# Full-height score and broadcast matmuls, and a last gated merge whose gate products run two tiles ahead

## The chip, the cores and the metric

The kernel runs on one core of a Trainium2 chip. The metric is the device time of one execution in microseconds (us), the median of several runs. The engines are TensorE (PE in the profile; its weight loads are listed apart as PEld), VectorE (DVE), ScalarE (ACT), GpSimd (POOL) and SyncE (SP), which issues the transfers.

## What is computed

A trunk of two layers over 256 latent tokens and 256 context tokens of width 1024, all in fp32. Each layer normalises and modulates its input, runs four branches of width 256 (a bidirectional mLSTM, differential attention, a Fourier mix and a spatial-gating MLP), projects each branch back to 1024, weighs it with a sigmoid gate, sums the four and projects the sum; then comes a gated feed-forward block. The parts that the change touches:

```python
def step(carry, inp):                      # mLSTM, one chunk of 128 tokens
    C, n, m = carry
    qc, kc, vc, ic, fc = inp
    b = jnp.cumsum(fc, axis=-1)
    dmat = jnp.where(tril, b[..., :, None] - b[..., None, :] + ic[..., None, :], -jnp.inf)
    inter = b + m[..., None]
    m_t = jnp.maximum(inter, jnp.max(dmat, axis=-1))
    wt = jnp.exp(dmat - m_t[..., None])
    ...
    s = jnp.einsum('bhtd,bhsd->bhts', qc, kc) * wt
    num = a[..., None] * jnp.einsum('bhvk,bhtk->bhtv', C, qc) + jnp.einsum('bhts,bhsv->bhtv', s, vc)

def merge(branches, gate_pre, w_branch, w_out):
    br = jnp.stack(branches, axis=2)
    y = jnp.einsum('bsgc,gcd->bsgd', br, w_branch)
    gt = jax.nn.sigmoid(gate_pre.reshape(gate_pre.shape[:2] + (N_BRANCH, D_MODEL)))
    return jnp.einsum('bsgd,bsgd->bsd', gt, y) @ w_out
```

The last layer computes its query side for the latent tokens alone.

## The kernel before

**Number form.** TensorE has no full-speed fp32 product here. A value is split into a high part (cast to the type fp32r) and a low part (what the cast dropped), and a product is three matmuls: high x high (line 135), high x low (136), low x high (137). `wload` (line 111) brings a weight tile of 128x1024 in over SyncE (`raw`), casts it on ScalarE (`hi`, line 122) and subtracts on VectorE or GpSimd (`lo`, line 131). There are four such buffers, and two more in layer 1.

**Tokens.** Activations lie with channels on the partitions and tokens along the columns. Layer 0 works on `TQ` = 512 columns (latent and context tokens), layer 1 on 256.

**mLSTM scores.** For each of the four heads of a layer the program builds weights `W` on VectorE and ScalarE from a broadcast tile `nb`, computes scores of queries and keys on TensorE, multiplies both on VectorE (`mulw`, line 1052), and sums over tokens with the values (`nu`, line 1092, plain fp32). A head is 64 channels, half the partitions. `split_pair` (lines 923 to 937) therefore packs the two parts of the key into one tile `k2`: the high part in the head's 64 partitions, the low part in the other 64. `q2` holds the query's high part twice. One 128-row matmul `k2` x `q2` then gives two of the three products (line 942), and a second one of 64 rows, `k2`'s high part x `ql`, the third (line 943). `ql`, the query's low part, is one tile for a pair of heads, each in its own 64 partitions. A head has four pairs of such matmuls: in layer 0 two with 256 columns and two with 512, in layer 1 four with 256.

**Broadcast.** `NM` holds a running minimum per head and direction, in rows 0 to 3 and 32 to 35. `NMr` (lines 998 to 1000) is its high and low part on 36 partitions. Line 1029 spreads one row over all 128 partitions: the left operand is a column of an identity matrix (`idr`) repeated 128 times. There are four such matmuls for a head, with `TQ` columns.

**Merge.** `merge(g)` goes over eight output tiles `m` of 128 channels: gate product `gt` (24 matmuls on `w_gate`), tanh on ScalarE into `sig`, branch product `yb` (6 matmuls on `w_branch`), `sig` times `yb`, sum into `za`. Three merges are done as a generator that `fill(n)` advances by `n` half tiles between the steps of the branches: branches 2, 3 and 0; the last, branch 1 (the attention), runs at the end of the mixer and also writes `z`, the operand pair of the output projection (`split_out`: high part on ScalarE, low part on VectorE). `finish_heads` (line 710 on) normalises a branch's heads and queues `turn_heads`, which transposes the result on TensorE (`pt`, line 725, plain fp32) and splits it into the operands `bh` (line 680, ScalarE) and `bl` (line 681, VectorE) of the branch product. `finish_now` runs what is queued. In the layer's end (lines 1341 to 1349) the program does two steps of merge 0, then `finish_now`, then the rest of merge 0, then the last merge.

**Order and buffers.** A scheduler sets the order of the instructions of each engine by the priority in which the program wrote them, and moves what is ready. Of PSUM's eight banks three are for `gt`, `yb` and the projections, five for the rest (`nb`, scores, `nu`, `pt`). In layer 0 VectorE also works off a list of adaLN rows (`junk`, line 232) for the feed-forward block, one with each merge tile.

Of the kernel before, what the change touches and what calls it, by code (L numbers as in the profile page):

```python
# [10 lines left out]
F32 = mybir.dt.float32  # L11
F32R = mybir.dt.float32r
I32 = mybir.dt.int32
AF = mybir.ActivationFunctionType
# [5 lines left out]
KD = 8  # L20
# [15 lines left out]
def trunk_kernel(ctx: ExitStack, tc: tile.TileContext, I, out):  # L36
# [25 lines left out]
    def mmb(name="mm"):  # L62
        return mmp.tile([128, 512], F32, tag="mm", name=name)
# [584 lines left out]
    def layer(l):  # L648
# [15 lines left out]
        with ExitStack() as es:  # L664
# [41 lines left out]
            def finish_heads(g, hs, t2, wmul, wbc, post):  # L706
# [22 lines left out]

                fins.append(turn_heads)  # L730

            def merge(g, first=False, final=False):
                wb = None
                for m in range(KD):

                    wt = wload(I["w_gate"][l, m, g])
                    if m % 4 == 0:
                        wb = wload(I["w_branch"][l, g, m // 4])
                    ps = mmb("gt")
                    gemm(ps[:, :TQ], wt, h, 0, TQ, ks=range(4), last=False)  # L740
                    if not final:
                        yield

                    gemm(ps[:, :TQ], wt, h, 0, TQ, ks=range(4, KD), w0=4, first=False)
                    sig = wk.tile([128, 512], F32, tag="sig", name="sig")[:, :TQ]
                    last_sig[0] = ins_of(nc.scalar.activation(out=sig, in_=ps[:, :TQ], func=AF.Tanh, scale=0.5))
                    ps = mmb("yb")
                    gemm(ps[:, :TQ], wb, br[g], 0, TQ, ks=range(2), w0=2 * (m % 4))
                    o = za[m] if first else sig
                    at = nc.vector.scalar_tensor_tensor(out=o, in0=sig, scalar=1.0, in1=ps[:, :TQ], op0=ALU.add,  # L750
                                                        op1=ALU.mult)
                    if not first:
                        (nc.vector if final else nc.gpsimd).tensor_tensor(out=za[m], in0=za[m], in1=sig, op=ALU.add)
                    if final:
                        split_out(z[m], za[m], 0.5)
                    tick(1, ins_of(at))
                    yield
# [10 lines left out]
            def fill(n):  # L768
                for _ in range(n):
                    while units:  # L770
                        if next(units[0], 0) is None:
                            break
                        units.pop(0)
# [110 lines left out]
            def mlstm():  # L884
# [4 lines left out]
                Bt = w2.tile([128, T], F32, name="mlB", tag="mlB")  # L889
                NM = w2.tile([128, T], F32, name="mlNM")  # L890
                sp = []
                uem = w2.tile([128, 2, 4, 64], F32, name="uem")
                nc.gpsimd.memset(Bt, 0.0)
                nc.gpsimd.memset(NM, 0.0)
                qk = []
# [27 lines left out]
                def split_pair(p):  # L923

                    aq, ak = qk[2 * p:2 * p + 2]
                    for hh in range(2):
                        o, x_ = slice(64 * hh, 64 * hh + 64), slice(64 - 64 * hh, 128 - 64 * hh)
                        if hh == 0:
                            ql = w2.tile([128, TQ], F32R, name="ql", tag="ql")
                        q2 = w2.tile([128, TQ], F32R, name="q2", tag=f"q2{hh}")  # L930
                        k2 = w2.tile([128, T], F32R, name="k2", tag=f"k2{hh}")
                        nc.scalar.copy(q2[o], aq[o])
                        nc.scalar.copy(k2[o], ak[o])
                        nc.scalar.copy(q2[x_], aq[o])
                        nc.vector.tensor_tensor(out=k2[x_], in0=ak[o], in1=k2[o].bitcast(F32), op=ALU.subtract)
                        nc.vector.tensor_tensor(out=ql[o], in0=aq[o], in1=q2[o].bitcast(F32), op=ALU.subtract)
                        sp.append((q2, k2, ql))

                def score(ps, j, n):
                    q2, k2, ql = sp[hd]  # L940
                    s = slice(j * 128, (j + 1) * 128)
                    nc.tensor.matmul(ps, k2[:, s], q2[:, 0:n], start=True, stop=False)
                    nc.tensor.matmul(ps, k2[pr, s], ql[pr, 0:n], start=False, stop=True)

                qk_tiles(0, CFG["qa"][l])

# [48 lines left out]
                                        op0=ALU.mult)  # L995
                nc.vector.tensor_copy(uem[:, 1, :, 0:36], pv_[:, 1, :, 0:36])

                NMr = [w.tile([128, T], F32R, name=f"NMr{i}", tag=tg)[0:36] for i, w, tg in ((0, w2, "mlB"), (1, w3, "mlU"))]
                nc.vector.tensor_copy(NMr[0][:, :TQ], NM[q, :TQ])
                nc.vector.tensor_tensor(out=NMr[1][:, :TQ], in0=NM[q, :TQ], in1=NMr[0][:, :TQ].bitcast(F32), op=ALU.subtract)  # L1000


                wo = w2.tile([128, NTQ, 256], F32, name="wo")
# [17 lines left out]
                for hd in range(4):  # L1021
# [3 lines left out]
                    for d in range(2):  # L1025
                        row = hd + 32 * d
                        nb = aux("nb")
                        for i in range(2):
                            nc.tensor.matmul(nb[:, :TQ], idr[0:36, row:row + 1].to_broadcast([36, 128]), NMr[i][:, :TQ],
                                             start=(i == 0), stop=(i == 1))  # L1030
                        W = w2.tile([128, 9 if last else 10, 128], F32, name="W", tag="W", bufs=CFG["W"])
                        mask = cst[:, C_MF:C_MF + 128] if d == 0 else cst[:, C_MB:C_MB + 128]
                        u = lambda j: uem[:, 0, j, row:row + 1]
                        for j in range(NTQ):
                            nc.vector.scalar_tensor_tensor(out=W[:, j, :], in0=nb[:, j * 128:(j + 1) * 128], scalar=u(j),
                                                           in1=mask, op0=ALU.add, op1=ALU.add)
                        nc.scalar.activation(out=W[:, 0:NTQ, :], in_=W[:, 0:NTQ, :], func=AF.Exp)
                        for j in (2, 3):
                            nc.scalar.activation(out=W[:, 2 * j:2 * j + 2, :].rearrange("p a b -> p (a b)"), in_=nb[:, 0:256],
                                                 func=AF.Exp, bias=u(j), scale=1.0)  # L1040
                        sj, tj = (0, 1) if d == 0 else (1, 0)
                        nc.scalar.activation(out=W[:, 8, :], in_=nb[:, tj * 128:(tj + 1) * 128], func=AF.Exp, bias=u(sj), scale=1.0)
                        if not last:
                            nc.scalar.activation(out=W[:, 9, :], in_=nb[:, (2 + tj) * 128:(3 + tj) * 128], func=AF.Exp,
                                                 bias=u(2 + sj), scale=1.0)
                        Ws.append(W)
# [292 lines left out]
                            for m in range(CFG["na"] if last else 16, 40))  # L1339
            diff(*(diff_tiles() if last else dqk))  # L1340
            es3.close()
            fill(CFG["f3"][l])
            finish_now()
            fill(64)
            G1 = mod_scale(vec, mod, 2, 1, False, ns)
            g1 = row_of(G1, "t1", RS) if last else None
            open_z()
            units.append(merge(1, final=True))
            fill(64)
            turn[1] = CFG["tw1"] if last else CFG["tw"]  # L1350
            es1.close()
# [237 lines left out]
def ins_of(i):  # L1589
    return i.ins if hasattr(i, "ins") else i  # L1590
# [79 lines left out]
```

## Time and profile before

| | us |
|---|---|
| median of three runs | 1425.84 |
| lowest and highest run | 1424.82, 1427.07 |
| the profiled execution, its own time | 1426.35 |
| its span in the trace | 1424.2 |
| TensorE busy in the span | 1356.0 (95%) |
| VectorE, ScalarE, GpSimd busy | 858.6, 621.5, 848.1 |

The span is what the hardware profiler saw from the first instruction to the last; some 2.2 us of the execution's time lie around it. Busy time of TensorE includes the overlap of a matmul with the next: a row's length is longer than the distance to the next row's start. Two stretches of mLSTM heads lie at 137 to 196 us (layer 0) and 990 to 1042 us (layer 1). The last merges run around 392 to 460 us and 1153 to 1190 us.

### The profile page before, as it was taken

How to read it: one execution, taken by the hardware profiler on the slowest of the kernel's cores; microseconds unless marked ns; L12 is line 12 of the kernel's file. 1: busy time of each engine (PE TensorE's matmuls, PEld its weight loads, DVE VectorE, ACT ScalarE, POOL GpSimd, SP SyncE). 2: the span in 40 equal slices, each digit the busy share in tenths (PEclk: the TensorE clock that was granted, in tenths of full speed). 3: DMA queues.
4: the chain of work that ended last, by engine and by line, in shares of the span. 5: the costliest groups of instructions: out<-in, count | busy, mean ns of one | idle time of the engine just before them, and what ended most of it. 6: DMA issues, size and time to landing. Idle time of an engine off the chain costs nothing.

```text
span 1424.2 us, 22769 instructions
## 1 busy us (share of the span) xinstructions
PE 1356.0 (95%) x8514; PEld 1201.4 (84%) x8514; DVE 858.6 (60%) x1554; ACT 621.5 (44%) x1098; POOL 848.1 (60%) x974
## 2 busy tenths in 40 slices
PE   8899999999999979999799999798999989899998
PEld 6597789888878969888588889797899988899997
DVE  4738655888785475599876643767637632533323
ACT  4445425443423555423231333466536544555543
POOL 1534133456764676567465545775356889678895
PEclk9999999999999999999899999998999999999999
DMA  9322123333443443465577533433224445355552
GB/s 345 133 103 76 45 69 124 133 134 134 162 149 113 149 158 110 143 227 192 206 248 256 186 123 104 132 122 113 90 75 134 136 161 180 118 192 193 182 188 74
DMA packets 61934, 210.55 MB, mean 148 GB/s; under 512 B 7144, under 2 KB 9728, under 8 KB 61568
## 3 DMA queue, kind: packets, MB, share of 16 engines
q1 hardware_dynamic: 61824, 209.10, 43.2%
q8 instruction: 67, 1.10, 0.3%
q14 instruction: 43, 0.35, 0.1%
HBM read 208.01 MB, written 1.06 MB: 147 GB/s over the span
## 4 chain that ended last, share of the span: by engine, by line
PE 53%; DVE 4%; POOL 3%; issue 2%; ACT 1%; DMA 1%; DVEq 0%; ACTq 0%; SPq 0%; POOLq 0%
PE ug L135 4%; PE ug L136 4%; PE ug L137 4%; PE ua L135 4%; PE ua L136 4%; PE ua L137 4%; PE o L135 3%; PE o L136 3%; PE o L137 3%; PE gt L135 2%; PE gt L137 2%; PE gt L136 2%; POOL lo L131 2%; PE ty L135 2%; PE ty L136 2%
## 5 line engine op out<-in xcount | busy, mean ns | idle before, releaser
L131 POOL TENSOR_TENSOR lo<-raw,hi 128x256 fp32r<-128x256 f32 x814 | 697.6, 889 | 409.9 <-ACT hi L122 383.9
L122 ACT CAST hi<-raw 128x1024 fp32r<-128x1024 f32 (+2 forms) x284 | 293.6, 1036 | 332.8 <-PE ua L136 76.9
L135 PE MATMUL gt<-hh,hi 128*128 128x512 f32 (+1 forms) x512 | 177.5, 347 | 0.0
L131 DVE TENSOR_TENSOR lo<-raw,hi 128x1024 fp32r<-128x1024 f32 (+2 forms) x79 | 120.7, 1527 | 90.2 <-ACT hi L122 90.2
L137 PE MATMUL gt<-hh,lo 128*128 128x512 f32 (+1 forms) x512 | 173.1, 338 | 0.0
L136 PE MATMUL gt<-hl,hi 128*128 128x512 f32 (+1 forms) x512 | 172.6, 337 | 0.0
L135 PE MATMUL ug<-hh,hi 128*128 128x256 f32 (+1 forms) x384 | 126.2, 329 | 11.7 <-DVE ca L1454 11.7
L232 DVE SCALAR_TENSOR_TENSOR ar<-ar,scb 128x1024 f32<-128x1024 f32 x80 | 123.0, 1542 | 18.4 <-DMA ar<-w_adaT 17.6
L136 PE MATMUL ug<-hl,hi 128*128 128x256 f32 (+1 forms) x384 | 125.5, 327 | 0.0
L135 PE MATMUL ua<-hh,hi 128*128 128x256 f32 (+1 forms) x384 | 124.5, 324 | 0.9 <-ACT hh L301 0.9
L137 PE MATMUL ug<-hh,lo 128*128 128x256 f32 (+1 forms) x384 | 125.2, 326 | 0.0
L136 PE MATMUL ua<-hl,hi 128*128 128x256 f32 (+1 forms) x384 | 124.1, 323 | 0.1
L137 PE MATMUL ua<-hh,lo 128*128 128x256 f32 (+1 forms) x384 | 124.0, 323 | 0.0
L135 PEld LDWEIGHTS gt<-hh,hi 128*128 128x128 f32 x512 | 96.9, 189 | 13.4 <-issue 2.5
L137 PEld LDWEIGHTS gt<-hh,lo 128*128 128x128 f32 x512 | 96.9, 189 | 10.7
L136 PEld LDWEIGHTS gt<-hl,hi 128*128 128x128 f32 x512 | 97.2, 190 | 9.7
L135 PEld LDWEIGHTS ug<-hh,hi 128*128 128x128 f32 x384 | 74.3, 193 | 18.5 <-issue 10.2
L135 PE MATMUL o<-fh,hi 128*128 128x256 f32 (+1 forms) x240 | 81.0, 338 | 0.0
L136 PE MATMUL mm<-lo,hh 128*128 128x256 f32 x272 | 78.8, 290 | 1.9 <-DVE lo L131 1.9
L136 PE MATMUL o<-fl,hi 128*128 128x256 f32 (+1 forms) x240 | 80.5, 336 | 0.0
L137 PE MATMUL o<-fh,lo 128*128 128x256 f32 (+1 forms) x240 | 80.5, 335 | 0.0
L135 PE MATMUL mm<-hi,hh 128*128 128x256 f32 x272 | 79.3, 292 | 0.0
(309 smaller groups left out, 3252.2 us busy)
## 6 DMA issues: line engine op xcount, KB each, us to landing
raw<-w_up SPq DMA_DIRECT2D x92, 512.0 KB, 3.6
ar<-w_adaT SPq DMA_DIRECT2D x80, 512.0 KB, 4.2
raw<-w_gate SPq DMA_DIRECT2D x64, 512.0 KB, 3.5
raw<-w_tm SPq DMA_DIRECT2D x24, 512.0 KB, 3.5
raw<-w_dr SPq DMA_DIRECT2D x22, 512.0 KB, 3.5
raw<-w_dn SPq DMA_DIRECT2D x20, 512.0 KB, 3.7
ada_w<-w_ada SPq DMA_DIRECT2D x16, 512.0 KB, 8.4
raw<-w_branch SPq DMA_DIRECT2D x16, 512.0 KB, 3.7
```

Source lines behind the costliest of these rows:

```text
L122: nc.scalar.copy(hi[:, :n], raw[:, :n])
L131: e.tensor_tensor(out=lo[:, s], in0=raw[:, s], in1=hi[:, s].bitcast(F32), op=ALU.subtract)
L135: nc.tensor.matmul(ps, a[0], b[0], start=start, stop=False)
L136: nc.tensor.matmul(ps, a[0], b[1], start=False, stop=False)
L137: return nc.tensor.matmul(ps, a[1], b[0], start=False, stop=stop)
L232: nc.vector.scalar_tensor_tensor(out=raw if st == ns - 1 else junk, in0=raw, scalar=0.5, in1=scb[:, st, :], op0=ALU.mult, op1=ALU.mult, ac ...
```

## The change

Three things are done together.

1. The second score matmul takes all 128 rows of `k2`, and `ql` is 128 rows high with zeros in the half that isn't the head's. For that there are two `ql` tiles per layer, one for each head of a pair, both made once; GpSimd writes the zeros ahead of the heads. The second pair no longer waits to overwrite a shared `ql`.
2. `NMr` has all 128 partitions and the broadcast takes all 128 rows of `idr`'s column. `uem` shrinks from 64 to 36 columns.
3. Merge 0 is finished first. The last merge becomes `merge_last`: the gate product and tanh of tile `m` are issued two tiles ahead of its branch product, and the first two gates stand ahead of the head transposes.

```diff
+            def merge_last(g):
+                sigs, wbs = {}, {}
+
+                def gate(m):
+
+                    wt = wload(I["w_gate"][l, m, g])
+                    ps = mmb("gt")
+                    gemm(ps[:, :TQ], wt, h, 0, TQ)
+                    sigs[m] = wk.tile([128, 512], F32, tag="sig", name="sig")[:, :TQ]
+                    last_sig[0] = ins_of(nc.scalar.activation(out=sigs[m], in_=ps[:, :TQ], func=AF.Tanh, scale=0.5))
+
+                def out(m):
+
+                    if m % 4 == 0:
+                        wbs[0] = wload(I["w_branch"][l, g, m // 4])
+                    ps = mmb("yb")
+                    gemm(ps[:, :TQ], wbs[0], br[g], 0, TQ, ks=range(2), w0=2 * (m % 4))
+                    sig = sigs.pop(m)
+                    at = nc.vector.scalar_tensor_tensor(out=sig, in0=sig, scalar=1.0, in1=ps[:, :TQ], op0=ALU.add,
+                                                        op1=ALU.mult)
+                    nc.vector.tensor_tensor(out=za[m], in0=za[m], in1=sig, op=ALU.add)
+                    split_out(z[m], za[m], 0.5)
+                    tick(1, ins_of(at))
+
+                ahead = 2
+                for m in range(KD + ahead):
+                    if m >= ahead:
+                        out(m - ahead)
+                    if m < KD:
+                        gate(m)
+                    yield
...
-                uem = w2.tile([128, 2, 4, 64], F32, name="uem")
+                qls = [w2.tile([128, TQ], F32R, name=f"ql{hh}", tag=f"ql{hh}") for hh in range(2)]
+                for hh in range(2):
+                    nc.gpsimd.memset(qls[hh][64 - 64 * hh:128 - 64 * hh].bitcast(F32), 0.0)
+                uem = w2.tile([128, 2, 4, 36], F32, name="uem")
...
-                        if hh == 0:
-                            ql = w2.tile([128, TQ], F32R, name="ql", tag="ql")
+                        ql = qls[hh]
...
-                    nc.tensor.matmul(ps, k2[pr, s], ql[pr, 0:n], start=False, stop=True)
+                    nc.tensor.matmul(ps, k2[:, s], ql[:, 0:n], start=False, stop=True)
...
-                NMr = [w.tile([128, T], F32R, name=f"NMr{i}", tag=tg)[0:36] for i, w, tg in ((0, w2, "mlB"), (1, w3, "mlU"))]
-                nc.vector.tensor_copy(NMr[0][:, :TQ], NM[q, :TQ])
-                nc.vector.tensor_tensor(out=NMr[1][:, :TQ], in0=NM[q, :TQ], in1=NMr[0][:, :TQ].bitcast(F32), op=ALU.subtract)
+                NMr = [w.tile([128, T], F32R, name=f"NMr{i}", tag=tg) for i, w, tg in ((0, w2, "mlB"), (1, w3, "mlU"))]
+                nc.vector.tensor_copy(NMr[0][:, :TQ], NM[:, :TQ])
+                nc.vector.tensor_tensor(out=NMr[1][:, :TQ], in0=NM[:, :TQ], in1=NMr[0][:, :TQ].bitcast(F32), op=ALU.subtract)
...
-                            nc.tensor.matmul(nb[:, :TQ], idr[0:36, row:row + 1].to_broadcast([36, 128]), NMr[i][:, :TQ],
+                            nc.tensor.matmul(nb[:, :TQ], idr[:, row:row + 1].to_broadcast([128, 128]), NMr[i][:, :TQ],
...
-            fill(CFG["f3"][l])
+            fill(64)
+            units.append(merge_last(1))
+            fill(2)
             finish_now()
-            fill(64)
             G1 = mod_scale(vec, mod, 2, 1, False, ns)
             g1 = row_of(G1, "t1", RS) if last else None
             open_z()
-            units.append(merge(1, final=True))
             fill(64)
```

In layer 0 the transposes `pt` move on TensorE. Before, they stand in the middle of a gate of merge 0 (`gt_3955`):

```order
L135 MATMUL gt_3955<-hh3_130,hi_3951 128x512
L136 MATMUL gt_3955<-hl3_131,hi_3951 128x512
L137 MATMUL gt_3955<-hh3_130,lo_3952 128x512
L725 MATMUL pt_3968<-cst_93,fsq_3902 128x128 x2
L725 MATMUL pt_3973<-cst_93,fsq_3902 128x128 x2
L725 MATMUL pt_3978<-cst_93,fsq_3911 128x128 x2
L725 MATMUL pt_3983<-cst_93,fsq_3911 128x128 x2
L135 MATMUL gt_3955<-hh4_132,hi_3951 128x512
```

After, on TensorE at the same step, they stand behind the second gate of the last merge (`gt_4088`), and the first branch product of the last merge (`yb_4165`) begins right behind them:

```order
L135 MATMUL gt_4088<-hh7_138,hi_4084 128x512
L136 MATMUL gt_4088<-hl7_139,hi_4084 128x512
L137 MATMUL gt_4088<-hh7_138,lo_4085 128x512
L725 MATMUL pt_4115<-cst_93,fsq_3904 128x128 x2
L725 MATMUL pt_4120<-cst_93,fsq_3904 128x128 x2
L725 MATMUL pt_4125<-cst_93,fsq_3913 128x128 x2
L725 MATMUL pt_4130<-cst_93,fsq_3913 128x128 x2
L135 MATMUL yb_4165<-bh0_2050,hi_4158 128x512
L135 MATMUL gt_4186<-hh0_124,hi_4182 128x512
L136 MATMUL gt_4186<-hl0_125,hi_4182 128x512
L137 MATMUL gt_4186<-hh0_124,lo_4183 128x512
L136 MATMUL yb_4165<-bl0_2051,hi_4158 128x512
```

The transposes have moved 96 matmuls back. `bh0` is written by the first and the third of the four casts, 256 columns each.

On ScalarE of layer 0 those casts stand, before, behind the tanh of an earlier gate (`gt_3886`):

```order
L122 CAST hi_4087<-raw_4085 128x1024
L746 ACTIVATE sig_3934<-gt_3886 128x512
L680 CAST bh0_2048<-pt_3968 128x256
L680 CAST bh1_2050<-pt_3973 128x256
L680 CAST bh0_2048<-pt_3978 128x256
L680 CAST bh1_2050<-pt_3983 128x256
```

After, on ScalarE, they stand behind the tanh of the gate just ahead of the transposes, and behind the cast of a weight tile (`hi_4281`) whose buffer is `gt_4088`'s:

```order
L122 CAST hi_4230<-raw_4228 128x1024
L741 ACTIVATE sig_4080<-gt_4055 128x512
L122 CAST hi_4281<-raw_4279 128x1024
L741 ACTIVATE sig_4113<-gt_4088 128x512
L680 CAST bh0_2050<-pt_4115 128x256
L680 CAST bh1_2052<-pt_4120 128x256
L680 CAST bh0_2050<-pt_4125 128x256
L680 CAST bh1_2052<-pt_4130 128x256
```

What moved: a weight cast and a tanh that both need `gt_4088` now stand between the transposes and their casts. In layer 1 the order is the same, with one cast for each of `bh0` and `bh1`, and two matmuls of a row sum (line 407) between the transposes and the first branch product.

## Rows read from the trace of the kernel before

**Rows 1.** The page, part 1: busy us (share of the span) and instructions.
```profile
PE 1356.0 (95%) x8514; PEld 1201.4 (84%) x8514; DVE 858.6 (60%) x1554; ACT 621.5 (44%) x1098; POOL 848.1 (60%) x974
```

**Rows 2.** The list of waits: us in total, times, longest us.
```profile
PE pt L725 <- DVE fsq L718: 6.5, 3, 3.8
...
DVE junk L232 <- DMA ar<-w_adaT: 9.8, 8, 3.9
```

**Rows 3.** TensorE's timeline, layer 0, head 0: start us, us, engine, line, operation.
```profile
137.64 0.28 PE L137 MATMUL mm<-hi,hl 128*128 128x256 f32 x1
...
139.31 0.40 PE L136 MATMUL gt<-hl,hi 128*128 128x512 f32 x1
...
141.83 0.28 PE L942 MATMUL SL<-q,k 128*128 128x256 f32 x1
142.04 0.38 PE L943 MATMUL SL<-ql,k 64*128 64x256 f32 x1
142.35 0.38 PE L942 MATMUL SL<-q,k 128*128 128x256 f32 x1
...
145.02 0.40 PE L136 MATMUL gt<-hl,hi 128*128 128x512 f32 x1
```

**Rows 4.** The weight loads' timeline of the same head.
```profile
141.60 0.19 PEld L942 LDWEIGHTS SL<-q,k 128*128 128x128 f32 x1
142.04 0.18 PEld L943 LDWEIGHTS SL<-ql,k 64*128 64x128 f32 x1 [0.25 <-issue]
```

**Rows 5.** TensorE's timeline, layer 1, head 0, around its scores.
```profile
996.80 0.28 PE L942 MATMUL SL<-q,k 128*128 128x256 f32 x1
...
999.42 0.28 PE L136 MATMUL gt<-hl,hi 128*128 128x256 f32 x1
```

**Rows 6.** Windows, layer 1's last merge: us, busy (x) PE PEld DVE ACT POOL, PEclk, DMA.
```profile
1159.00:1160.00 1.00, 1.00 (x7) 1.00 (x6) 0.00 (x0) 0.43 (x1) 0.19 (x1) 0.50 0.21 66
1170.00:1190.00 20.00, 20.00 (x170) 20.00 (x169) 9.19 (x19) 10.41 (x18) 16.74 (x22) 1.00 0.49 164
```

**Rows 7.** VectorE's timeline, layer 1, head 0: first and last products with W.
```profile
998.13 0.62 DVE L1052 SCALAR_TENSOR_TENSOR W<-SL,W 128x256 f32<-128x256 f32 x2 [1.53 <-PE SL L943]
...
999.88 0.75 DVE L1052 SCALAR_TENSOR_TENSOR W<-SC,W 128x256 f32<-128x256 f32 x2
```

**Rows 8.** TensorE's timeline of the same head, the sum over tokens.
```profile
1001.85 1.34 PE L1092 MATMUL nu<-v,W 128*128 128x65 f32 x11
```

**Rows 9.** TensorE's timeline, layer 0, around the head transposes.
```profile
392.61 0.39 PE L137 MATMUL gt<-hh,lo 128*128 128x512 f32 x1
394.79 0.63 PE L725 MATMUL pt<-cst,fsq 128*128 128x128 f32 x4 [1.79 <-DVE fsq L718]
...
396.30 0.47 PE L135 MATMUL gt<-hh,hi 128*128 128x512 f32 x1
396.62 0.39 PE L136 MATMUL gt<-hl,hi 128*128 128x512 f32 x1
```

**Rows 10.** TensorE's timeline, layer 1, around the head transposes.
```profile
1153.27 0.28 PE L136 MATMUL gt<-hl,hi 128*128 128x256 f32 x1
...
1159.07 0.41 PE L136 MATMUL gt<-hl,hi 128*128 128x256 f32 x1
1159.28 0.41 PE L137 MATMUL gt<-hh,lo 128*128 128x256 f32 x1
...
1161.82 0.28 PE L136 MATMUL gt<-hl,hi 128*128 128x256 f32 x1
```

**Rows 11.** ScalarE's timeline, layer 0, behind a later gate of the last merge.
```profile
454.32 1.05 ACT L122 CAST hi<-raw 128x1024 fp32r<-128x1024 f32 x1 [3.03 <-PE gt L136]
455.27 0.59 ACT L746 ACTIVATE sig<-gt 128x512 f32<-128x512 f32 x1
```

**Rows 12.** TensorE's timeline, the last matmul of that gate.
```profile
454.07 0.39 PE L137 MATMUL gt<-hh,lo 128*128 128x512 f32 x1
```

**Rows 13.** ScalarE's timeline, layer 0: casts behind the head transposes.
```profile
395.23 0.65 ACT L680 CAST bh<-pt 128x256 fp32r<-128x256 f32 x2 [4.92 <-PE pt L725]
```

## The prediction

> **What bounds the kernel now.** I read the page's list of engines first: TensorE is busy for 95% of the span [rows 1], so only what makes TensorE's own row of work shorter, or fills its idle time, can move the end. The list of waits comes second: around the change TensorE waits in one place, the head transposes of line 725 [rows 2]; the list has no wait of TensorE in the two mLSTM stretches (137 to 196 us and 990 to 1042 us). There I read TensorE's timeline matmul by matmul, because "busy" hides how far apart they start. The unit is the pitch, the time from one start to the next in a run of equal matmuls. With 512 columns, 11 starts lie between 139.31 and 141.83 [rows 3], 0.229 us each; with 256 columns a long stretch of the merge has 170 in 20 us, 0.118 us each, at a granted clock of 1.00 [rows 6]. Whatever stands further apart than that is what an edit could win.
>
> **Scores, 128 rows instead of 64.** From the first score to the second matmul of the gate behind it, layer 0 takes 141.83 to 145.02 [rows 3]: 3.19 us for eight score matmuls (four of 256 columns, four of 512) and one gate matmul. At the pitch they would take 4x0.118 + 5x0.229 = 1.62, so 1.57 us per head are lost. In layer 1 it is 996.80 to 999.42 [rows 5]: 2.62 us for nine matmuls of 256 columns, which want 1.06; 1.56 lost. The reason that I read is in the weight loads [rows 4]: the 128-row load begins 0.23 us ahead of its matmul at 141.83, while the 64-row load begins at 142.04, with its own matmul [rows 3]. A load that isn't ahead puts its 0.18 us into TensorE's row, and the next 128-row load isn't ahead of a 64-row matmul either: the third score starts at 142.35 [rows 3], 0.31 later. With all operands 128 rows high these loads are like the gates' loads. I therefore take the whole loss: 4x1.57 + 4x1.56 = 12.5 us. Bounds: nothing (rival 1) and 12.5.
>
> The work that this needs elsewhere: two memsets per layer on GpSimd, ahead of any score; the second pair's `ql` is computed a head earlier on VectorE, since its buffer is no longer shared. I cost both at nothing; TensorE doesn't wait there, and the loss would show as a wait of scores, which sits in rival 2.
>
> **Broadcast of NM, 128 rows instead of 36.** Head 0 of layer 0: from the last projection matmul to the second gate matmul is 137.64 to 139.31 [rows 3], 1.67 us for one matmul of 256 and five of 512 columns, which want 1.26: 0.41 lost. Six of the eight heads have plain fp32 matmuls (`nu`) just ahead instead of a gemm, and part of their loss is that switch, which stays: behind the plain fp32 transposes of the merge a gate matmul takes 0.32 (396.30 to 396.62 [rows 9]) instead of 0.229. For these I take half, 0.21. Sum: 2x0.41 + 6x0.21 = 2.1 us; bounds 0 and 8x0.41 = 3.3. The cast and the subtraction that make `NMr` run over the same number of columns on more partitions; I cost that at nothing, and the 36-column `uem` too.
>
> **What becomes late in mLSTM.** Each head's `nu` matmuls need the products `W` times score of line 1052 on VectorE. In layer 1 the last of them ends at 999.88 + 0.75 = 1000.63 [rows 7], `nu` starts at 1001.85 [rows 8]: 1.22 us of slack. TensorE will arrive 1.56 us earlier, but the products also start earlier: the first waited for the scores [rows 7], and those come 0.6 us earlier (four matmuls from 996.80 end near 997.4 instead of 998.0). So 1.8 us of lead (1.22 + 0.6) stand against 1.56; I take 0.3 us for all heads together, and the case in which the products start no earlier as rival 2. mLSTM: 12.5 + 2.1 - 0.3 = 14.3 us.
>
> **Last merge, layer 0.** Now TensorE does half a gate, waits for the heads, transposes, and waits again: 392.61 to 396.62 [rows 9] is 4.01 us for two gate matmuls (0.46) and eight transposes. Four of these take 0.63 us with their tail [rows 9], which I read as a pitch of 0.095, so 0.76; lost 2.8. After the change 96 matmuls (22 us) stand between, so the transposes' input is long there, but the order shows the new wait: TensorE's next matmul behind the transposes reads `bh0`, whose casts stand on ScalarE behind a weight cast and a tanh that wait for gate 1 itself. The same pair stands in a later gate: the gate's last matmul starts at 454.07 [rows 12], the weight cast at 454.32, the tanh at 455.27 [rows 11], 0.95 later; it frees ScalarE some 0.53 later; three casts at half of 0.65 each [rows 13] make 0.98. So `bh0` is ready 0.25 + 0.95 + 0.53 + 0.98 = 2.7 us after that start; TensorE is through with matmul and transposes after 0.23 + 0.76 = 1.0. New wait 1.7, gain 1.1. At the end the last two `yb` stand together, so two `z` instead of one are finished late; I take 0.4 us for that, most of one more ScalarE instruction on 512 columns (the tanh's 0.53 above). Net gain 0.7. Bounds: -2, if an adaLN row blocks VectorE's `bl` for as long as the longest wait of its kind, 3.9 us [rows 2], and +2.8.
>
> **Last merge, layer 1.** 1153.27 to 1161.82 [rows 10] is 8.55 us. In it are 18 matmuls of 256 columns (2.12), four transposes (0.38) and two row sums (about 0.5); lost 5.5 us. 3.8 of it is the longest wait of [rows 2]; most of the rest is the clock, 0.50 in the stretch from 1159 [rows 6], that is 1.2 instead of 2.4 GHz after TensorE had stood still, with a pitch of 0.213 (1159.07 to 1159.28 [rows 10]). The new wait by the same chain: 0.25 + 0.95 + at most 0.53 for the tanh + one cast of 0.33 = 2.05 us after the gate's last start, against 0.12 + 0.38 + 0.5 = 1.0 for TensorE. New wait 1.1, too short, I judge by layer 0's gaps, to bring the half clock. Gain 4.4; bounds 1.7 (the new wait becomes as long as the old one's 3.8) and 5.5.
>
> **Sum.** 14.3 + 0.7 + 4.4 = 19.4 us off the profiled execution: 1426.35 (span 1424.2, 2.2 around it) - 19.4 = 1406.95. This execution is 0.5 above the median of the runs, so 1406.4.
>
> **Rivals.**
> 1. Widening does nothing. The 64-row load takes 0.18 us and the 128-row one 0.19 [rows 4]: equal, so if the 0.31 between scores comes from anything but the change of height, the scores and broadcasts stay as they are. The Trainium skill, "TensorE: Matmul & The Clock Gate", section "LDWEIGHTS (loading the stationary operand)", speaks for this one: the time of a load goes by its columns, not by its contraction rows. The trace agrees on the lengths of single loads, 0.18 and 0.19 us. Against it stands where the loads start. It loses the 14.6 us of the two parts and returns the 0.3: 1406.4 + 14.3 = 1420.7. Chance 0.05.
> 2. A wait for `W` takes the place. If ScalarE's exponentials hold the products where they are, `nu` would find them ready at 1000.63 plus some 0.2, and TensorE would stand there at 1001.85 - 1.56 = 1000.29: 0.55 us per head, 4.4 for eight, less the 0.3 counted: 1410.5. The same for the gain of the broadcast could add 2. Chance 0.15. For: little slack. Against: the first product waits for the score now.
> 3. The merge pipeline gives nothing: the casts behind the weight cast cost what the old wait cost, and the half clock comes back. The 5.1 us go: 1411.5. Chance 0.14.
> 4. Slower: TensorE now runs the four heads without gaps, and the chip grants it 1.2 GHz there. At a pitch of 0.213 instead of 0.118 each microsecond of work costs 0.8 more, so 25 us of such work use up the gain. If layer 1's mLSTM stretch (52 us, some 45 after the change) ran so, it would add 36: 1442. Against: the merge at 1170 to 1190 runs without a gap at 1.00 [rows 6]. Chance 0.03.
>
> **How the numbers follow.** My forecast, 1406.4, has 0.63. With all upper bounds it ends at 12.5 + 3.3 + 2.8 + 5.5 = 24.1 us, 1401.8; with the lower bounds of the two merges at 1406.4 + 2.7 + 2.7 = 1411.8. To hold 8 in 10 the range takes in rivals 2 and 3: 1401.5 to 1412. About 0.2% (2.9 us) is what a measurement can tell from no change. Forecast and rivals 1 to 3 are all faster by more; only rival 1 with rival 3 reaches "same". Faster 0.95, same 0.02, slower 0.03.
>
> **What would show it.** Scores and gates at one pitch (eight scores and one gate matmul in about 1.6 us in layer 0, 1.1 in layer 1); the `ql` loads ahead of their matmuls; five matmuls from the broadcast in 1.15 to 1.3 us. In the merges: a wait of TensorE for `bh` on ScalarE of 1 to 2 us, none for `fsq`, and a granted clock of 1.00 through layer 1's. Waits of `nu` for `W` of 0.5 us per head would prove rival 2; an unchanged pitch of 0.31 rival 1.

## The result and the profile after

The changed kernel takes 1408.34 us (median; 1407.98 to 1410.11 in four runs), the kernel before 1425.57 in the runs beside it. The ratio is 0.9872 with a 95% interval of 0.9855 to 0.9889: 15.8 to 20.7 us faster. The forecast was 1406.4 with a range of 1401.5 to 1412. The profiled execution's span went from 1424.2 to 1406.2 us.

The page's first part; TensorE's busy time fell by 19.1 us [rows 1], VectorE's rose by 5.2, and those of ScalarE and GpSimd stayed within 2 us:

```profile
PE 1336.9 (95%) x8514; PEld 1195.1 (85%) x8514; DVE 863.8 (61%) x1554; ACT 621.6 (44%) x1098; POOL 849.7 (60%) x978
```

TensorE's timeline in layer 0, head 0, which answers to [rows 3] (line numbers are 32 to 34 higher below the new function):

```profile
139.61 0.28 PE L137 MATMUL mm<-hi,hl 128*128 128x256 f32 x1
139.73 1.09 PE L1063 MATMUL nb<-NMr,idr 128*128 128x512 f32 x4
...
140.88 0.40 PE L136 MATMUL gt<-hl,hi 128*128 128x512 f32 x1
...
143.43 0.28 PE L976 MATMUL SL<-q,k 128*128 128x256 f32 x1
143.55 0.28 PE L977 MATMUL SL<-ql,k 128*128 128x256 f32 x1
143.67 0.28 PE L976 MATMUL SL<-q,k 128*128 128x256 f32 x1
...
145.07 0.39 PE L136 MATMUL gt<-hl,hi 128*128 128x512 f32 x1
```

From the first score to the second gate matmul it is 143.43 to 145.07, 1.64 us instead of 3.19; the scores stand 0.12 apart like any other matmul. From the last projection matmul to the second gate matmul it is 139.61 to 140.88, 1.27 instead of 1.67. The loads of the same head, which answer to [rows 4], now all begin ahead of their matmuls, `ql`'s at 143.44 for 143.55:

```profile
143.20 0.19 PEld L976 LDWEIGHTS SL<-q,k 128*128 128x128 f32 x1
143.44 0.19 PEld L977 LDWEIGHTS SL<-ql,k 128*128 128x128 f32 x1
```

In layer 1 the nine matmuls of [rows 5] take 988.28 to 989.36, 1.08 us instead of 2.62:

```profile
988.28 0.28 PE L976 MATMUL SL<-q,k 128*128 128x256 f32 x1
...
989.36 0.28 PE L136 MATMUL gt<-hl,hi 128*128 128x256 f32 x1
```

TensorE's waits in the last merges (us in total, times, longest), first layer 0 with the start of the output projection, then layer 1:

```profile
PE yb L135 <- ACT bh L680: 1.4, 1, 1.4
PE o L136 <- DVE zl L684: 0.9, 2, 0.7
```

```profile
PE yb L135 <- ACT bh L680: 1.6, 1, 1.6
PE gt L135 <- DVE sig L782: 1.0, 1, 1.0
PE gt L137 <- POOL lo L131: 0.6, 1, 0.6
```

The waits for `fsq` of [rows 2] are gone from both merges. In their place stand the forecast waits for `bh`, and three that the prediction didn't have as waits of their own: for `zl` in layer 0, for `sig` and for a weight's `lo` in layer 1.

All times below by stage are differences of starts in TensorE's timeline: "heads" from the first `nb` to the first score `ds` of the attention (before: 137.86 to 238.06 and 994.61 to 1068.83), "to the projection" from there to the first matmul of the output projection (462.60 and 1190.25), "first block" from there to the first matmul of the norm's sums (`st`). Stages repeat within some 0.2 us where a kernel doesn't touch them, with two exceptions: layer 0's way to the projection (224.5 or 226.0) and layer 1's (121.4 to 124.0). Both go with the granted clock, layer 1's in part with a wait as well, as shown at the end of the section on the prediction.

| us | heads 0 | heads 1 | to the projection 0 | first block 0 | to the projection 1 |
|---|---|---|---|---|---|
| before | 100.20 | 74.22 | 224.54 | 23.01 | 121.42 |
| changed | 92.57 | 66.88 | 223.36 | 24.19 | 120.10 |
| scores alone | 93.88 | 67.98 | 226.01 | 23.18 | 121.51 |
| broadcast alone | 98.88 | 72.92 | 224.54 | 23.18 | 122.31 |
| merge alone | 100.20 | 74.21 | 223.95 | 24.19 | 120.07 |
| scores and broadcast | 92.58 | 66.90 | 224.46 | 23.00 | 121.47 |

### The profile page after: what moved, and what is told of

It reads as the page before. It is cut to its first block, busy times and chain, and to the rows that moved or that the text cites. A ratio compares the mean times of both kernels' runs of the same rounds, so it can differ in the third digit from the quotient of the medians.

```text
span 1406.2 us, 22765 instructions
## 1 busy us (share of the span) xinstructions
PE 1336.9 (95%) x8514; PEld 1195.1 (85%) x8514; DVE 863.8 (61%) x1554; ACT 621.6 (44%) x1098; POOL 849.7 (60%) x978
## 5 line engine op out<-in xcount | busy, mean ns | idle before, releaser
L136 PE MATMUL ua<-hl,hi 128*128 128x256 f32 (+1 forms) x384 | 124.0, 323 | 0.1
L135 PEld LDWEIGHTS ua<-hh,hi 128*128 128x128 f32 x384 | 72.8, 190 | 7.6 <-ACT hh L301 1.1
```

Of the source, the lines that this page charges most:

```text
L135: nc.tensor.matmul(ps, a[0], b[0], start=start, stop=False)
L136: nc.tensor.matmul(ps, a[0], b[1], start=False, stop=False)
```

## Experiments: the parts alone

**Scores alone.** The edit is the change without its lines on `NMr`, `nb` and the merge:

```diff
...
-                    nc.tensor.matmul(ps, k2[pr, s], ql[pr, 0:n], start=False, stop=True)
+                    nc.tensor.matmul(ps, k2[:, s], ql[:, 0:n], start=False, stop=True)
```

> Only the scores of the change: the second score matmul takes 128 rows, two zero-filled low-part query tiles; broadcast and last merge as before. Theory 1 (a change of height between neighbouring matmuls costs TensorE some 0.2 us, and nothing waits for the products behind): the eight heads give the predicted 12.5 us, so 1413 against 1425.5, and score matmuls stand at 0.118 and 0.229. Theory 2 (the products with W on VectorE become the bound): TensorE shows waits of the token sums of about 0.5 us a head, and only some 8 us are gained, 1417.5.

Measured: 1413.12 us, ratio 0.9907 (0.9893 to 0.9921). The heads' stages fall by 6.32 and 6.24, 12.56 us together: theory 1. TensorE's one wait in these stages, 0.9 us for `fsq` behind the heads of layer 1, stands in the kernel before too.

**Broadcast alone.** The edit is the second part of the change but for `uem`.

```diff
...
-                            nc.tensor.matmul(nb[:, :TQ], idr[0:36, row:row + 1].to_broadcast([36, 128]), NMr[i][:, :TQ],
+                            nc.tensor.matmul(nb[:, :TQ], idr[:, row:row + 1].to_broadcast([128, 128]), NMr[i][:, :TQ],
```

> Only the broadcast of the change: 128 rows of the identity column and of NM; scores and last merge as before. Theory 1: 2.1 us faster, 1423.4; bounds 0 and 3.3. If the loss at the broadcast were that of plain fp32 matmuls ahead alone, nothing: 1425.5.

Measured: 1423.24 us, ratio 0.9973 (0.9961 to 0.9985). The heads' stages fall by 1.32 and 1.30, 2.62 us: more than the 2.1, inside the bounds. In the heads behind plain fp32 matmuls, the stretch from the last `nu` to the second gate matmul went from 1.66 us to 1.32 in layer 0 (from 153.27 to 154.93 before).

**Both.**

> Scores and broadcast at 128 rows, the last merge as before. Theory 1: the sum of both alone, 14.3 to 14.6 us faster, 1411. If slack of the products with W runs out only where both are done, less than the sum of the two alone by up to 4 us: 1415.

Measured: 1411.37 us, ratio 0.9893 (0.9877 to 0.9909). The stages fall by 7.62 and 7.32, 14.94 us, 0.24 less than the two parts alone.

**Merge alone.**

> Only the last merge of the change, with gates two tiles ahead; scores and broadcast as before. As predicted it would be 5.1 us faster: 1420.4. By what is left of the whole change's 17.2 us after 14.3 for the two other parts, 2.9: 1422.6. If waits that only the joined kernel has (for a PSUM bank ahead of gate 1, for a weight's low part in layer 1) eat it, this kernel alone comes nearer to 1420.4 than to 1422.6.

Measured: 1423.43 us, ratio 0.9974 (0.9963 to 0.9985), 2.1 to 5.3 us faster. By stages it is less: 0.6 gained on layer 0's way to the projection, 1.2 lost in the first block, 1.35 gained in layer 1. The waits in layer 1 are those of the changed kernel, within 0.05 us, so joining the parts is not what made them: they belong to the merge. What the profiled execution gains beyond the stages lies outside them: 1.1 us of it in the feed-forward of layer 1, behind the merge, where the half clock was granted for a shorter stretch (see the sum below).

## Experiments: why full height helps

**Every second pair in the other order.** The 64-row matmuls stay; the pairs with odd `j` do the 64-row matmul first, so that two of one height meet:

```diff
-                    nc.tensor.matmul(ps, k2[:, s], q2[:, 0:n], start=True, stop=False)
-                    nc.tensor.matmul(ps, k2[pr, s], ql[pr, 0:n], start=False, stop=True)
+                    def whole(first):
+                        nc.tensor.matmul(ps, k2[:, s], q2[:, 0:n], start=first, stop=not first)
+
+                    def half(first):
+                        nc.tensor.matmul(ps, k2[pr, s], ql[pr, 0:n], start=first, stop=not first)
+
+                    for i, f in enumerate((whole, half) if j % 2 == 0 else (half, whole)):
+                        f(i == 0)
```

> The kernel before, with its 64-row matmuls kept and the two matmuls of every second score pair in the other order (64 rows first), so that a head has four changes of height between neighbouring matmuls instead of eight. Theory 1 (the change of height costs, some 0.2 us each): 0.78 us a head, 6.3 in all: 1419.3 against 1425.5. Theory 2 (a 64-row matmul costs in itself): 1425.5, none gained.

TensorE's timeline of head 0 of layer 0:

```profile
143.15 0.28 PE L943 MATMUL SL<-q,k 128*128 128x256 f32 x1
143.36 0.50 PE L946 MATMUL SL<-ql,k 64*128 64x256 f32 x2
143.79 0.39 PE L943 MATMUL SL<-q,k 128*128 128x256 f32 x1
```

Two 64-row matmuls of 256 columns now take 143.36 to 143.79, 0.43 for two where each took 0.31 before. The heads' stages fall by 3.14 (100.20 to 97.06) and 2.74 (74.22 to 71.48), 5.9 us of the 6.3 that theory 1 gives. The time is 1423.73 us, ratio 0.9968 (0.9958 to 0.9977), 4.6 us faster by the ratio, with layer 1's way to the projection 2.6 us longer in the profiled execution, where nothing was edited: the granted clock was 0.50 there from 1154 to 1158 us and 0.60 to 1160, and TensorE waited 1.2 us for `sig`, a wait that the trace of before doesn't have.

**Both matmuls of 64 rows.**

```diff
-                    nc.tensor.matmul(ps, k2[:, s], q2[:, 0:n], start=True, stop=False)
+                    nc.tensor.matmul(ps, k2[pr, s], q2[pr, 0:n], start=True, stop=False)
```

> The kernel before, with the first score matmul cut to 64 rows too: it leaves out the product of the key's low part with the query's high part. All eight score matmuls of a head then have one height, and only the two ends change it. Theory 1 (the change of height costs): the matmuls inside a head stand at 0.118 and 0.229 us, and some 1.2 us a head go, 9.4 in all: 1416. Theory 2 (a 64-row load can never start ahead of its matmul): the pitch inside a head stays at 0.31 and the time at 1425.5 or above.

```profile
143.98 0.39 PE L137 MATMUL gt<-hh,lo 128*128 128x512 f32 x1
144.30 0.38 PE L942 MATMUL SL<-q,k 64*128 64x256 f32 x1
144.52 0.28 PE L943 MATMUL SL<-ql,k 64*128 64x256 f32 x1
144.64 0.28 PE L942 MATMUL SL<-q,k 64*128 64x256 f32 x1
144.76 0.28 PE L943 MATMUL SL<-ql,k 64*128 64x256 f32 x1
```

Inside the group, 64-row matmuls start 0.12 us apart, like 128-row ones. The cost sits at the change: 0.32 from the gate's last matmul (0.09 over its pitch) and 0.22 from the first 64-row one (0.10 over). The loads show the same: the first 64-row load begins with its own matmul, the next one 0.11 us ahead.

```profile
144.30 0.18 PEld L942 LDWEIGHTS SL<-q,k 64*128 64x128 f32 x1 [0.35 <-issue]
144.41 0.19 PEld L943 LDWEIGHTS SL<-ql,k 64*128 64x128 f32 x1
```

The heads' stages fall by 4.66 and 4.30, 8.96 of the 9.4 expected; the time is 1418.81 us, ratio 0.9936 (0.9921 to 0.9951). So a 64-row matmul costs nothing beyond a 128-row one; each change of height between neighbours costs some 0.2 us, and the 128-row form pays because it removes eight of them from a head.

## Experiments: where the merge's gain went

**Layer 1, three waits.** TensorE's timeline of the changed kernel, which answers to [rows 10]:

```profile
1139.64 0.28 PE L137 MATMUL yb<-bh,lo 128*128 128x256 f32 x1
1140.94 0.38 PE L135 MATMUL gt<-hh,hi 128*128 128x256 f32 x1 [1.03 <-DVE sig L782]
...
1147.26 0.39 PE L407 MATMUL row<-cst,ms 128*8 128x128 f32 x2
1149.22 0.40 PE L135 MATMUL yb<-bh,hi 128*128 128x256 f32 x1 [1.58 <-ACT bh L680]
```

The first gate of the last merge waits for a bank of PSUM that VectorE's product `sig` (line 782) frees. VectorE's timeline shows that product behind the heads' scaling, which waited for GpSimd:

```profile
1139.34 1.22 DVE L716 TENSOR_TENSOR fsq<-dh,rs_y 128x512 f32<-128x512 f32 x1 [1.75 <-POOL rs_y L151]
1140.48 0.41 DVE L782 SCALAR_TENSOR_TENSOR sig<-sig,yb 128x256 f32<-128x256 f32 x1
```

So the wait for the heads has not gone; it comes back a gate earlier, through VectorE's queue. The second wait is the forecast one, but ScalarE's timeline names another releaser for the weight cast ahead of the `bh` casts. In [rows 11] it was the gate; here it is a transfer:

```profile
1147.58 1.04 ACT L122 CAST hi<-raw 128x1024 fp32r<-128x1024 f32 x1 [2.21 <-DMA raw<-w_branch]
1148.53 0.38 ACT L741 ACTIVATE sig<-gt 128x256 f32<-128x256 f32 x1
1148.81 0.64 ACT L680 CAST bh<-pt 128x256 fp32r<-128x256 f32 x2
```

That transfer was issued at 1143.99. It brings the second `w_branch` tile, which output tile 4 needs: behind it SyncE issues just two `w_gate` tiles, those of gates 6 and 7, and then the output projection's weights. SyncE's queue waited for GpSimd's low parts, which free the buffers (six waits between 1126 and 1150). GpSimd is busy without a gap (windows: us, busy of PE, PEld, DVE, ACT, POOL, granted clock, DMA):

```profile
1143.99 0.33 SPq L114 DMA_DIRECT2D raw<-w_branch  x1
```

```profile
SPq L114 <- POOL lo L131: 21.8, 6, 6.7
```

```profile
1141.00:1144.00 3.00, 3.00 (x25) 3.00 (x26) 2.37 (x3) 0.44 (x1) 3.00 (x4) 1.00 0.02 5
1144.00:1147.00 3.00, 3.00 (x28) 3.00 (x27) 0.00 (x0) 1.33 (x2) 3.00 (x5) 1.00 0.58 173
1147.00:1149.00 2.00, 0.64 (x5) 0.18 (x3) 0.62 (x2) 1.42 (x3) 2.00 (x4) 1.00 0.22 37
```

**The product ahead of the scaling.** In layer 1 the two scalings are issued behind `sig` of merge 0's seventh tile:

```diff
...
+                held = last and g == 1
+                if not held:
+                    scale()
 
                 def turn_heads():
 
+                    if held:
+                        with after(ats[-2]):
+                            scale()
...
```

> The changed kernel, with one order changed on VectorE in layer 1: the heads' last two scalings of the attention branch are issued behind the product with sig of merge 0's seventh tile, which otherwise stands behind them. Theory 1 (the wait of 1.2 us ahead of the last merge's first gate is for the PSUM bank that this product frees, and the product was late because VectorE stood at the scaling, which waited for GpSimd): that wait goes, about 1.2 us, of which the transposes may give back up to 0.5, since their input comes later. Theory 2 (TensorE's wait there is for something else, such as a weight): it stays at 1.2. Time 1407.1 against 1408.3, to be read from the trace.

The wait for `sig` is gone, so its cause was the one named. But the time stayed at 1408.80 us, ratio 0.9882 (0.9866 to 0.9898), and layer 1's way to the projection became 1.44 us longer, 121.54. TensorE came earlier to the same late weight:

```profile
1147.20 0.39 PE L135 MATMUL yb<-bh,hi 128*128 128x256 f32 x1 [2.79 <-ACT bh L680]
```

```profile
1145.56 1.04 ACT L122 CAST hi<-raw 128x1024 fp32r<-128x1024 f32 x1 [2.40 <-DMA raw<-w_branch]
```

The wait grew by 1.2 us, from 1.58 to 2.79, about as much as had been won; what the stage lost on top goes with the granted clock, which fell behind that wait:

```profile
1147.00:1149.00 2.00, 1.80 (x11) 1.80 (x12) 1.60 (x3) 0.42 (x2) 2.00 (x2) 0.72 0.94 375
1149.00:1151.00 2.00, 2.00 (x11) 2.00 (x11) 0.61 (x2) 0.00 (x0) 0.92 (x2) 0.50 0.37 135
```

**The branch weight earlier.** The first `w_branch` tile is loaded between the two gates' weights:

```diff
-                    if m % 4 == 0:
+                    if m == 4:
                         wbs[0] = wload(I["w_branch"][l, g, m // 4])
...
+                    if m == 1:
+                        wbs[0] = wload(I["w_branch"][l, g, 0])
```

> The changed kernel, with the first branch weight of the last merge loaded between the two gates' weights instead of behind both. In layer 1 the changed kernel's cast of that weight began when its transfer landed, and the branch operand's casts stood behind it. Theory 1: with the transfer earlier the wait in layer 1 falls from 1.6 to about 1.0 us (what is left is the tanh and the casts), 0.6 us in all: 1407.7 against 1408.3, too small to be told by the time, to be read from the trace. Theory 2: the second gate's weight is then the late one, and the wait stays or stands ahead of the second gate.

The expectation took the late weight for the first `w_branch` tile; it is the second, which this edit leaves where it was. The first tile's transfer did move, from 69.2 to 63.1 us behind the attention's first score in layer 1 at 1053.28 and 1053.58 (the changed kernel, then this one):

```profile
1122.51 0.33 SPq L114 DMA_DIRECT2D raw<-w_branch  x1
```

```profile
1116.72 0.33 SPq L114 DMA_DIRECT2D raw<-w_branch  x1
```

The second tile's transfer stands 90.7 us behind that score in both kernels, the cast ahead of `bh` still begins when it lands, and the wait for `bh` is 1.44 instead of 1.58 us. The time is 1409.74 us, ratio 0.9872 (0.9853 to 0.9891); layer 0's way to the projection is 0.7 us longer. So this run tests neither theory for the weight that was late; an earlier transfer of the second tile was not tried.

**The transposes between the gates.**

```diff
-            fill(2)
+            fill(1)
             finish_now()
+            fill(1)
```

> The changed kernel, with the head transposes of the last merge put between its first two gates instead of behind both, so that the second gate (5.5 us in layer 0, 2.8 us in layer 1) stands between the transposes and the first branch product. Theory 1 (the two new waits of TensorE for the casts of the branch operand, 1.4 and 1.6 us, are a matter of place): both go, about 3 us faster than the changed kernel, 1405 to 1406 where that one has 1408.3; in layer 1 the heads' input is there about 2 us before the first gate ends, so no wait for it comes back. Theory 2 (the casts are late because of the weights on their way, whatever the place): TensorE waits for them behind the second gate, and the time stays at 1408.

Both waits for `bh` are gone. Layer 0's way to the projection is 221.81 (1.55 shorter than in the changed kernel), layer 1's 118.83 (1.27 shorter), and TensorE's wait for a late low part in layer 1 is 0.9 instead of 0.6. The time is 1406.96 us, ratio 0.9856 (0.9839 to 0.9872) against 0.9872 for the changed kernel: the trace's 2.8 us fit, but the two intervals overlap.

**Branch product 6 ahead of gate 7.**

```diff
-                    if m >= ahead:
+                    if ahead <= m < KD:
                         out(m - ahead)
+                    if m == KD - 1:
+                        out(KD - ahead)
                     if m < KD:
                         gate(m)
+                    if m > KD:
+                        out(KD - 1)
```

> The changed kernel, with the last merge's branch product 6 issued ahead of gate 7 instead of behind it, so that only one z is late at the end. Theory 1 (two late z cost the output projection of layer 0 its 1.0 us): the first block of the projection falls from 24.2 to about 23.1 us, and TensorE's waits for zl there, 0.9 us, go; 1407.3 against 1408.3. Theory 2 (the projection's start is slower for another reason, such as weights): it stays at 24.2.

The first block of layer 0's projection is 23.06 instead of 24.19, and TensorE has no wait for `zl` there: the 1.1 us were the two late `z`. The time is 1408.04 us, ratio 0.9873 (0.9858 to 0.9888), which alone couldn't show it.

**The three edits joined**, and then with the low parts in layer 1's last merge shared evenly (in the second kernel):

```diff
+            if last:
+                turn[1] = 0.5
             units.append(merge_last(1))
```

> The changed kernel with three edits: head transposes between the last merge's first two gates, branch product 6 ahead of gate 7, and merge 0's product ahead of the heads' scaling on VectorE in layer 1. If the three waits are independent, 3 (transposes' casts) + 1.0 (z) + 1.2 (PSUM bank) less what GpSimd's late weight parts take back in layer 1 (0.7 to 1.1 us, seen in both kernels there): about 4 us below the changed kernel, 1404.5. If they only hand the wait on, 1407 as with the first edit alone.

> The joined kernel, and in layer 1's last merge every second weight's low part on VectorE instead of two in five. If GpSimd's queue is what TensorE waits for behind the third or fourth gate (0.6 to 0.9 us in the kernels so far), that wait goes: 0.9 us below the joined kernel. If VectorE becomes late with the branch operand or sig instead, it is as much slower.

The joined kernel takes 1405.59 us, ratio 0.9863 (0.9847 to 0.9878). Layer 0 has what was expected (221.74, first block 23.05). In layer 1 the waits are handed on once more, now to GpSimd, in full; layer 1's way to the projection is 119.16, longer than with the transposes' place alone:

```profile
PE gt L137 <- POOL lo L131: 1.9, 1, 1.9
```

With the low parts shared that wait is gone too, one of 1.2 us for `sig` has come at an earlier tile, and the stage is 117.61, the shortest of all. The kernel takes 1403.60 us (1402.85 to 1406.42), ratio 0.9847 (0.9833 to 0.9862): by the medians the fastest, 4.7 us below the changed kernel, though its interval still meets that one's end; that GpSimd's share is what made the last difference rests on the stage and the wait, since the joined kernel's interval overlaps too.

## Why the prediction was right, and where it was off

**Scores: right in size and reason.** 12.5 was forecast, 12.56 measured; rival 1 falls. The Trainium skill, "TensorE: Matmul & The Clock Gate", section "LDWEIGHTS (loading the stationary operand)", has the time of a load go by its columns; the lengths in the trace agree (0.18 and 0.19 us). The time was not in the lengths but in where a load starts at a change of height. The prediction tied the loss to 64-row loads that aren't ahead; among themselves they are, and 64-row matmuls run at full pitch.

**Broadcast: too small.** 2.62 instead of 2.1. The step that was off is the half taken for the six heads behind plain fp32 matmuls: in layer 0 each won 0.34 us there instead of 0.21.

**Lateness in mLSTM: near in size, the reason not shown.** 0.24 is lost to the joining of both, nearly all of it in layer 1; 0.3 was forecast. But TensorE has no wait of `nu` for `W` in any of these kernels, so that the 0.24 is lateness of `W` is not shown. In layer 1 VectorE's last product, which answers to [rows 7], ends 0.22 us before `nu` [rows 8] starts; the lead worked out was about 0.2. Rival 2 did not come, but little slack is left:

```profile
990.84 0.74 DVE L1086 SCALAR_TENSOR_TENSOR W<-SC,W 128x256 f32<-128x256 f32 x2
```

```profile
991.80 2.23 PE L1126 MATMUL nu<-v,W 128*128 128x65 f32 x19
```

**Layer 0's merge: 0.7 forecast, nothing measured.** The way to the projection is 1.18 shorter, which is the forecast gain of 1.1; the new wait, 1.38 us, is somewhat below the 1.7. The term that failed is the end, 0.4 for the late `z`: the first block is 1.18 longer, which the edit of the order gave back.

**Layer 1's merge: 4.4 forecast, 1.3 measured. This is the term that failed.** The old loss was read rightly, and the half clock of [rows 6] is gone, as forecast (granted clock 1.00 in all three windows above). What was wrong is that a wait taken off TensorE's row was taken to be gone. I priced the casts by layer 0, where the weights had long landed, and did not follow the weight cast to its transfer, nor the transfer to GpSimd, which works without a gap there; in the trace of before it was already busy for 18.9 of the 19 us from 1140 to 1159. Nor did I follow VectorE's queue from the heads' scaling to the PSUM bank of the next gate. The three waits of the changed kernel make 1.0 + 1.6 + 0.6 = 3.2 us in TensorE's list and 1.2 + 1.9 + 0.8 = 3.9 in that of its weight loads, where the prediction had one of 1.1: 2.8 us more, most of the 3.1 that are missing. Rival 3 came halfway: the waits' place, without its clock.

**Sum.** The stages give 14.94 + 0.0 + 1.32 = 16.3 us; the runs gave 17.2 with an interval of 15.8 to 20.7. The profiled execution's 18.0 has besides +1.9 up to the first head, -2.4 from the end of layer 0's first block to the heads of layer 1, and -1.1 behind the last merge. The first two scatter as much among kernels that don't touch them (137.85 to 140.89 at the first `nb`; 505.7 to 509.0 for the second stretch), so I put them down to no cause. The -1.1 lies in the feed-forward of layer 1, where the granted clock is 0.50 from 1224 to 1230 us before; after the change it is 0.72 from 1207 to 1209, 0.50 to 1211 and 0.93 to 1213. All six kernels with the old merge took the longer way there (233.6 to 234.1 us from the projection to the end), four of the eight with the new one the shorter (232.8) and four lay between or with the old (233.1 to 233.9). That the merge did it is not shown. Part of the total's nearness to the forecast is thus luck: the terms miss by 3.1 us, and stretches that no term was for gave back 1.7.

**Two lengths of the same stage.** Layer 0's way to the projection takes 224.5 us in four kernels with the old merge and 226.0 in two, the scores alone and the mirrored pairs. TensorE waits alike at the head transposes, 1.79 [rows 9] and 0.51 us before, 1.69 and 0.51 in the scores alone; but behind these waits the granted clock stayed at 1.00 in the first trace and fell in the second (a row of the windows before, then of the timeline and the windows of the scores alone):

```profile
396.00:398.00 2.00, 2.00 (x11) 1.71 (x12) 1.97 (x4) 0.65 (x2) 1.91 (x2) 1.00 0.32 63
```

```profile
389.15 0.63 PE L725 MATMUL pt<-cst,fsq 128*128 128x128 f32 x4 [1.69 <-DVE fsq L718]
```

```profile
392.00:394.00 2.00, 2.00 (x7) 1.58 (x6) 2.00 (x1) 0.00 (x0) 1.01 (x1) 0.56 0.92 321
```

In layer 1 every kernel with the old merge has a half clock behind the 3.8 us wait, in a shorter stretch in the trace of before (121.4) and in a longer one in the mirrored pairs (124.0, with the wait of 1.2 us for `sig`). So the 1.3 us that the changed kernel gained there are counted from the short one. Why the clock fell in one trace and not in the other is open.

## What to carry to other kernels

Where matmuls of different heights alternate, read the distance between their starts: it can pay to fill the short operand with zeros, or to put those of one height side by side, as each change cost 0.2 us here. Before a wait is priced as gone, follow the waiting work back until an engine or a transfer is found that has no gap; if there is one (GpSimd here), moving work ahead may only move the wait, as the product ahead of the scaling did, and taking work off that engine is what helped last. The place of a consumer can still matter: the transposes between the gates ended two waits. And when an order is moved ahead at the start of a loop, look at its end too: what was two tiles ahead there comes two at a time at the end.

## What was unexpected in the hardware

The cost of a change of height falls on both sides of it: 0.09 us over the pitch at the matmul before and 0.10 at the first one after, whichever height comes first; within a run of 64-row matmuls there is none.

The length of a standstill did not settle what the granted clock did. It stayed at 1.00 behind waits of 1.6 us (the changed kernel) and 1.9 us (the joined one) and fell to 0.50, that is 1.2 GHz, behind one of 2.8 us (the product ahead of the scaling), as it had behind 3.8 us before [rows 6]. But behind two waits of 1.7 to 1.8 and 0.5 us with four transposes between them, in layer 0, it stayed at 1.00 in four kernels and fell in two, which cost their stage 1.5 us. A stage's time is therefore compared only after a look at its granted clock.
